# The output projection of a hybrid encoder layer, in two parts: the SSD's half of the contraction for all tokens, then the heads' half by token halves

## The chip, the core and the metric

The kernel runs on one core of a Trainium2 chip. A core has TensorE (PE: matmuls, with its weight loads listed as PEld), VectorE (DVE), ScalarE (ACT), GpSimd (POOL) and SyncE (SP, which only issues transfers here). Matmuls write PSUM, a small memory of eight banks; everything else lives in SBUF, and tensors too large for it lie in HBM and come and go by DMA. The metric is the device time of the whole program in microseconds.

## The reference

One inference step of one encoder layer over 2048 new frames of a prompt and 32 frames of a running stream, width 1024. The mixer reads the normalised input through one projection; half of the result goes to eight heads of stick-breaking attention, the other half to a Mamba-2 state-space part (SSD). Both results are normalised, laid side by side and go through one output projection; a gated feed-forward with a short convolution follows.

```python
attn = stick_breaking(q, q_pos, k_all, v_all, k_pos).reshape(b, l, D_ATT)      # D_ATT = 512
...
y = rmsnorm(y * jax.nn.silu(z), p['g_ssm_out'])                                # D_SSM = 512
out = jnp.concatenate([rmsnorm(attn, p['g_attn_out']), y], axis=-1) @ p['w_out']
...
m, k, v, h_fin, ssm_conv_new = mixer(rmsnorm(x, p['g_mix_pre']), ...)
x = x + rmsnorm(m, p['g_mix_post'])
f, ffn_conv_new = conv_ffn(rmsnorm(x, p['g_ffn_pre']), ffn_conv_prev, p)
x = x + rmsnorm(f, p['g_ffn_post'])
```

All of it is in 32-bit floats. The kernel gets that accuracy from a faster matmul format by splitting both operands into a high and a low part: each product is three matmuls (high x high, high x low, low x high).

## The kernel before

**Tiling.** Features lie on the 128 partitions, tokens along the free dimension. The tokens are cut into four super-blocks of 512, 512, 512 and 544 (`SBS`). A contraction over 1024 features is eight chunks k of 128; of the output projection's input `cat`, chunks 0 to 3 are the heads and 4 to 7 the SSD's result.

**Stages.** First, `phase_in` projects all super-blocks and does the SSD; the SSD's normalised result is stored to HBM (`yS`). Then `heads(s)` does the attention of super-block s in slots (head, key chunk, query block): score matmuls (line 811), sigmoids on ACT (659, 660), a scan on DVE (662), a product mostly on POOL (667), transposes on PE (832), a copy (835) and the value matmuls (847). Between slots, `fill` draws steps from a generator, the dense work of the super-block before: `Tail.stream`. A step is one call of `dense`, three matmuls on line 124. `count` says how many steps a stream has, and `heads` spreads them over its slots. For the last super-block there are no heads left, and its stream runs alone (`alone`), with three PSUM buffers instead of two and token tiles of 272.

**A stream**, in order: `norm_in` (called when the heads are done) loads the SSD's half of `cat` from `yS` into buffers that the previous stream's up matmuls read until their end (line 753), sums and roots the heads' squares, and writes the normalised heads in two token halves (759 to 761). Then eight steps of `owed`, the down projection's rest that the previous super-block left (32 steps of three matmuls of 512 columns; none at super-block 0). Then `out_units` for the first token half, then for the second, with the steps of `residual` for the first half strewn in, one after each fourth yield. Then the root of the first half, the residual of the second, `split` of both halves into the up projection's operands (958, 959), the rest of `owed`, and the feed-forward.

**The projection.** A unit of `out_units` is one output chunk c for one token half: eight steps, SSD chunks first, into one PSUM buffer, then an ACT copy into `m[c]` (924) and its square added to `msq` by ACT and POOL through one buffer `sqt` (771, 772). Each chunk's weights are one tile `w` of 1 MB, high and low parts; three such buffers exist (`WBUFS`). The second half starts with the last three chunks, whose weights are still there, and loads the other five again. At super-block 0 the weights come raw, are split by ACT and POOL (108, 109) and stored (`wS_out`); later they are loaded from there (104). `residual` loads the layer's input (`xr`, 939, two buffers), scales and adds (940, 944), stores the sum (945) and squares it.

**Order of the work.** The tile framework lays out each engine's queue from a simulated time line, so instructions can move against the program's order where nothing forbids it. `pin` and `mark` keep the dense matmuls behind the attention matmuls that stand before them in the program; attention matmuls are not held back by dense ones. SP's queue runs in order.

## Time and profile before

| | |
|---|---|
| median of 3 runs | 3005.11 us (2995.95 to 3006.34) |
| profiled execution | 2999.56 us, span of its instructions 2997.4 us, 43276 instructions |
| mean granted TensorE clock | 0.979 |
| PE busy | 2839.3 us, 95% of the span |
| DVE / ACT / POOL busy | 1567.7 / 1239.6 / 1254.8 us |
| moved by DMA | 571.58 MB, mean 191 GB/s |

The time of an execution is its span and a little over 2 us around it. A busy PE is not PE at its peak: matmuls overlap, and a matmul's row is longer than the distance to the next. The output projections' ACT copies (line 924) lie at 772.1 to 834.0, 1302.9 to 1355.6, 1880.1 to 1933.7 and 2478.7 to 2524.1 us.

### The profile page before, as it was taken

Reading aid. Unit: us, or ns where it says so; the run is one execution under the profiler, and the core shown is the slowest. Engines: PE = TensorE matmul, PEld = TensorE weight load, DVE = VectorE, ACT = ScalarE, POOL = GpSimd, SP = SyncE. Lnnn points to the kernel's source line nnn. Section 1 sums busy time; section 2 is a strip of 40 time slices with the busy share of each in tenths; the row PEclk is TensorE's granted clock in tenths of the full one; section 3 lists DMA queues with packets and bytes.
Section 4 is the critical chain, followed back from the end, with each engine's and each line's share of the span. In section 5 each row is a group of like instructions: output and inputs, shape, how many; then the busy total and the mean of one; then the engine's idle time right before and its main releaser. Section 6 shows DMA issues by size and latency. Waiting matters only on the chain.

```text
span 2997.4 us, 43276 instructions
## 1 busy us (share of the span) xinstructions
PE 2839.3 (95%) x16175; PEld 2320.3 (77%) x16175; DVE 1567.7 (52%) x2386; ACT 1239.6 (41%) x2514; POOL 1254.8 (42%) x1077
## 2 busy tenths in 40 slices
PE   8999899989979999999999999999999999899996
PEld 6777778866757778886677777856777779799996
DVE  7676676546574544337734344485444543523334
ACT  5344444346675544337533333564333433312111
POOL 4555555245666665536522222454122224511113
PEclk9999999989989999999999999999999999899998
DMA  5645453657657777876455545645544455554555
GB/s 172 183 145 177 144 169 106 185 150 248 241 178 242 246 250 266 289 265 203 158 190 176 184 156 208 232 163 174 177 165 167 157 196 191 192 188 167 178 178 171
DMA packets 234659, 571.58 MB, mean 191 GB/s; under 512 B 49514, under 2 KB 101362, under 8 KB 205906
## 3 DMA queue, kind: packets, MB, share of 16 engines
q1 hardware_dynamic: 234450, 568.81, 57.2%
q8 instruction: 129, 2.11, 0.3%
q14 instruction: 80, 0.66, 0.1%
HBM read 435.22 MB, written 133.50 MB: 190 GB/s over the span
## 4 chain that ended last, share of the span: by engine, by line
PE 72%; DVE 14%; DMA 6%; issue 3%; ACT 3%; POOL 2%; SPq 1%; DVEq 0%; POOLq 0%; ACTq 0%
PE o L124 36%; PE u L124 11%; PE t L124 10%; PE pa L847 4%; PE z L811 3%; PE pt L832 3%; DVE prow L662 2%; PE o L365 2%; DVE xc L341 2%; DVE acB L436 1%; DMA xr<-hS 1%; DMA acB<-acD 1%; DVE xc L337 1%; DVE x L263 1%; DMA w<-wS_out 1%
## 5 line engine op out<-in xcount | busy, mean ns | idle before, releaser
L124 PE MATMUL o<-xhi,w 128*128 128x512 f32 (+2 forms) x3968 | 1039.6, 346 | 28.4 <-ACT xhi L287 7.9
L124 PEld LDWEIGHTS o<-xhi,w 128*128 128x128 f32 x3968 | 696.5, 191 | 129.6 <-issue 10.1
L124 PE MATMUL o<-xlo,w 128*128 128x512 f32 (+2 forms) x1984 | 684.9, 345 | 9.4 <-DVE xlo L959 4.1
L109 POOL TENSOR_TENSOR w<-wraw,w 128x1024 fp32r<-128x1024 f32 (+2 forms) x156 | 370.6, 2376 | 256.1 <-ACT w L108 233.3
L124 PEld LDWEIGHTS o<-xlo,w 128*128 128x128 f32 x1984 | 379.6, 191 | 56.8 <-DVE xlo L959 7.6
L667 POOL TENSOR_TENSOR beta<-beta,prow 128x512 f32<-128x512 f32 (+3 forms) x256 | 255.7, 1000 | 377.4 <-DVE prow L662 345.2
L124 PE MATMUL u<-xhi,w 128*128 128x512 f32 x1056 | 345.8, 398 | 0.8 <-ACT r L201 0.5
L124 PE MATMUL o<-ah,w 128*128 128x512 f32 x992 | 335.9, 401 | 3.3 <-ACT f L1057 2.6
L1013 POOL TENSOR_TENSOR y<-y,gb 128x512 f32<-128x512 f32 (+1 forms) x88 | 115.5, 1313 | 511.2 <-ACT gb L1012 509.2
L662 DVE TENSOR_TENSOR_SCAN prow<-gam,prow,z 128x513 f32<-128x513 f32 x192 | 244.8, 1277 | 108.7 <-ACT beta L660 103.2
L124 PEld LDWEIGHTS u<-xhi,w 128*128 128x128 f32 x1056 | 198.5, 188 | 56.1 <-issue 5.6
L659 ACT ACTIVATE gam<-z 128x512 f32<-128x512 f32 (+2 forms) x320 | 173.3, 542 | 128.1 <-PE z L811 83.0
L124 PEld LDWEIGHTS o<-ah,w 128*128 128x128 f32 x992 | 187.1, 189 | 49.8 <-ACT f L1057 3.6
L124 PE MATMUL u<-xlo,w 128*128 128x512 f32 x528 | 209.3, 396 | 0.0
L835 ACT COPY wt<-pt 128x512 f32<-128x512 f32 (+3 forms) x282 | 148.1, 532 | 144.0 <-PE pt L832 141.3
L1005 DVE SCALAR_TENSOR_TENSOR y<-gb,cv,y 128x512 f32<-128x512 f32 (+1 forms) x176 | 162.3, 923 | 78.4 <-ACT y L1003 75.6
L108 ACT CAST w<-wraw 128x1024 fp32r<-128x1024 f32 (+2 forms) x156 | 155.2, 995 | 114.5 <-PE o L124 63.7
L124 PE MATMUL o<-al,w 128*128 128x512 f32 x496 | 196.5, 396 | 0.0
L124 PE MATMUL t<-xhi,w 128*128 128x272 f32 x960 | 189.1, 292 | 2.3 <-DMA w<-wS_up 2.0
L832 PEld LDWEIGHTS pt<-ident,beta 128*128 128x128 f32 x1088 | 132.4, 144 | 67.8 <-issue 27.5
L832 PE MATMUL pt<-ident,beta 128*128 128x128 f32 x1088 | 177.4, 282 | 6.4 <-POOL beta L667 3.9
L124 PE MATMUL t<-ah,w 128*128 128x272 f32 (+1 forms) x768 | 160.1, 302 | 17.4 <-ACT f L1057 7.5
(262 smaller groups left out, 4845.9 us busy)
## 6 DMA issues: line engine op xcount, KB each, us to landing
w<-wS_up SPq DMA_DIRECT2D x132, 1024.0 KB, 4.8
w<-wS_dn SPq DMA_DIRECT2D x72, 768.0 KB, 4.8
wS_up<-w SPq DMA_DIRECT2D x44, 1024.0 KB, 4.8
w<-wS_out SPq DMA_DIRECT2D x39, 1024.0 KB, 6.3
wraw<-wup SPq DMA_DIRECT2D x44, 512.0 KB, 5.9
k<-kS SPq DMA_DIRECT2D x80, 256.0 KB, 4.0
wS_dn<-w SPq DMA_DIRECT2D x24, 768.0 KB, 4.5
w<-wS_dn SPq DMA_DIRECT2D x32, 512.0 KB, 4.4
```

The lines of the kernel that those rows point to most:

```text
L108: nc.scalar.copy(hi[:, :n, :], raw[:, :n, :])
L109: nc.gpsimd.tensor_tensor(lo[:, :n, :], raw[:, :n, :], hi[:, :n, :].bitcast(F32), op=ALU.subtract)
L124: mm = nc.tensor.matmul(ps[:, : c1 - c0], l[:, k, :], at(r, k0 + k)[:, c0:c1], start=first and i == 0 and k == 0, stop=last and i == 2 and ...
L659: nc.scalar.activation(g[:, c0:512], z, AF.Sigmoid, scale=-0.125)
L662: nc.vector.tensor_tensor_scan(back(pr), back(g), z[:, 0:1].to_broadcast([P, n + 1]), self.kn.ones[:, 0:1] if prev is None else prev, op0= ...
L667: eng.tensor_tensor(b[:, :n], b[:, :n], pr[:, c0 + 1 : 513], op=ALU.mult)
L811: mm = nc.tensor.matmul(z[:, :n], q[:, P * b : P * b + P], k[:, :n], start=e == 0, stop=e == 1 and kc < s)
L832: mm = nc.tensor.transpose(t[:, P * j : P * j + P], w[:, P * j : P * j + P], kn.ident[:])
L835: copy(wt[:, : n // P, P * b : P * b + P], t[:, :n].rearrange("p (i q) -> p i q", q=P))
L847: nc.tensor.matmul(av[DH * (j % 2) : DH * (j % 2) + DH, c0:], v[:, j, :], wt[:, j, c0:], start=kc == s and j < 2, stop=kc == 0 and j > 1,)
L1005: nc.vector.scalar_tensor_tensor(y[:, :W], gb[:, i : i + W], kn.col(wc + i), y[:, :W], op0=ALU.mult, op1=ALU.add)
L1013: nc.gpsimd.tensor_tensor(y[:, :W], y[:, :W], t, op=ALU.mult)
```

## The change

`out_units` is cut in two. A new `out_ssd` runs first, over all tokens of the super-block in tiles of up to 512: for each output chunk four steps (SSD chunks 4 to 7), then an ACT copy into `m[c]`. It stands where the eight owed steps stood; all owed steps now come behind the split. `out_units` keeps the heads' four chunks by token halves; DVE adds their PSUM result to `m[c]` in place, and the squares follow. The weights are laid out anew, two output chunks' halves to a 1 MB tile: four tiles for the SSD (`wouts`), four for the heads (`wouta`), of which the second token half reloads one. Residual steps come after each second yield instead of each fourth, since the second half has half as many. `count` follows.

```diff
+    def out_ssd(self, s, cat):
+        kn, nc, att = self.kn, self.kn.nc, self.att
+        self.m = [self.mp.tile([P, 544], F32, name=f"m{c}") for c in range(KC)]
+        self.msq = att.tmp.tile([P, 544], F32, name="msq")
+        self.w = {}
+        for c in range(KC):
+            if c % 2 == 0:
+                w = kn.weight(kn.wp, kn.a["wouts"][c // 2], key=("outs", c // 2))
+            for c0, c1 in tiles_of(SBS[s][1]):
+                ps = self.po[0].tile([P, 512], F32, name=self.po[1])
+                for k in range(4):
+                    j = c % 2 * 4 + k
+                    kn.dense(ps, [t[:, j : j + 1, :] for t in w], cat, c0, c1, ks=1, k0=4 + k, first=k == 0, last=k == 3, pin=self.pin)
+                    if k < 3:
+                        yield
+                nc.scalar.copy(self.m[c][:, c0:c1], ps[:, : c1 - c0])
+                yield
...
     def out_units(self, s, cat, half):
...
-        back = list(range(KC - WBUFS, KC))
-        for i, c in enumerate(range(KC) if c0 == 0 else back + list(range(KC - WBUFS))):
...
-            for k in (4, 5, 6, 7, 0, 1, 2, 3):
...
-            nc.scalar.copy(m[:, c0:c1], ps[:, : c1 - c0])
-            att.square(self.msq[:, c0:c1], m[:, c0:c1], i == 0)
-            yield
+        for i, p in enumerate(range(4) if c0 == 0 else (1, 2, 3, 0)):
+            w = self.w.pop(p, None)
             if w is None:
+                pool = self.keep if self.keep is not None and p == 0 else kn.wp
+                w = kn.weight(pool, kn.a["wouta"][p], key=("outa", p), tag="w0" if pool is self.keep else None)
+                if c0 == 0 and (p or pool is self.keep):
+                    self.w[p] = w
+            for c in (2 * p, 2 * p + 1):
+                m = self.m[c][:, c0:c1]
+                ps = self.po[0].tile([P, 512], F32, name=self.po[1])
+                for k in range(4):
+                    j = c % 2 * 4 + k
+                    kn.dense(ps, [t[:, j : j + 1, :] for t in w], cat, c0, c1, ks=1, k0=k, first=k == 0, last=k == 3, pin=self.pin)
+                    if k < 3:
+                        yield
+                nc.vector.tensor_tensor(m, ps[:, : c1 - c0], m, op=ALU.add)
+                att.square(self.msq[:, c0:c1], m, i == 0 and c % 2 == 0)
+                yield
...
-        yield from islice(owed, 8)
+        yield from self.out_ssd(s, cat)
         yield from self.out_units(s, cat, a)
         chain = self.residual(s, a)
         for n, _ in enumerate(self.out_units(s, cat, b)):
             yield
-            if n % 4 == 0:
+            if n % 2 == 0:
                 next(chain, None)
...
-        return 2 * 8 * 8 + (2 * NJ * 8 + NJ * 8) * len(tiles_of(SBS[s][1])) - (32 if s == 0 else 0)
+        return 64 + (32 + 2 * NJ * 8 + NJ * 8) * len(tiles_of(SBS[s][1])) - (16 if s == 0 else 0)
...
+    def pairs(w):
+        return c(w.reshape(4, 2, P, 4, P).transpose(0, 2, 1, 3, 4).reshape(4, P, KC, P))
...
-        "wout": units(i["w_out"][0]),
+        "wouta": pairs(wout[:, :, :4]),
+        "wouts": pairs(wout[:, :, 4:]),
```

More of the change, by code (lines that the diff above doesn't have):

```diff
@@ L1 @@
 from contextlib import ExitStack
-from itertools import islice
 import concourse.bass as bass
@@ L905, in out_units @@
         c0, c1 = half
-        if c0 == 0:
-            self.m = [self.mp.tile([P, 544], F32, name=f"m{c}") for c in range(KC)]
-            self.msq = att.tmp.tile([P, 544], F32, name="msq")
-            self.w = {}
-        back = list(range(KC - WBUFS, KC))
-        for i, c in enumerate(range(KC) if c0 == 0 else back + list(range(KC - WBUFS))):
-            m = self.m[c]
-            w = self.w.pop(c, None)
-            if w is None:
-                pool = self.keep if self.keep is not None and c not in back else kn.wp
-                w = kn.weight(pool, kn.a["wout"][c], key=("out", c), tag=f"w{c}" if pool is self.keep else None)
-                if c0 == 0 and (c in back or pool is self.keep):
-                    self.w[c] = w
-            ps = self.po[0].tile([P, 512], F32, name=self.po[1])
-            for k in (4, 5, 6, 7, 0, 1, 2, 3):
-                kn.dense(ps, [t[:, k : k + 1, :] for t in w], cat, c0, c1, ks=1, k0=k, first=k == 4, last=k == 3, pin=self.pin)
-                if k != 3:
-                    yield
-            nc.scalar.copy(m[:, c0:c1], ps[:, : c1 - c0])
-            att.square(self.msq[:, c0:c1], m[:, c0:c1], i == 0)
-            yield
+        for i, p in enumerate(range(4) if c0 == 0 else (1, 2, 3, 0)):
+            w = self.w.pop(p, None)
+            if w is None:
+                pool = self.keep if self.keep is not None and p == 0 else kn.wp
[13 more added lines that the diff above has]
+                yield
     def residual(self, s, half):
@@ L1218, in fm @@
         return v.reshape(-1, P).T
+    def pairs(w):
+        return c(w.reshape(4, 2, P, 4, P).transpose(0, 2, 1, 3, 4).reshape(4, P, KC, P))
     i = {k: np.asarray(v) for k, v in inp.items()}
+    wout = units(i["w_out"][0])
     w_in = i["w_in"][0]
```

## The prediction

> **What bounds the kernel now.** I read the page's busy times first, then busy time by stretches around each output projection, then the same stretches for line 124 alone (the dense matmuls), then the PE timeline, the chain and the waits.
>
> ```profile
> PE 2839.3 (95%) x16175; PEld 2320.3 (77%) x16175; DVE 1567.7 (52%) x2386; ACT 1239.6 (41%) x2514; POOL 1254.8 (42%) x1077
> 1000.00:1250.00 250.00, 250.00 (x1115) 195.93 (x1115) 118.34 (x135) 108.56 (x191) 149.94 (x92) 1.00 0.75 258
> 736.00:763.00 27.00, 20.80 (x124) 13.26 (x123) 22.54 (x31) 19.92 (x44) 19.96 (x21) 1.00 0.55 182
> 763.00:806.00 43.00, 42.49 (x302) 36.75 (x303) 21.66 (x27) 29.54 (x70) 34.05 (x34) 0.92 0.67 242
> 834.00:876.00 42.00, 32.58 (x163) 18.55 (x161) 31.04 (x40) 30.10 (x72) 25.87 (x31) 0.88 0.53 169
> 1285.00:1297.00 12.00, 7.76 (x39) 6.20 (x38) 5.51 (x11) 3.42 (x8) 6.89 (x8) 0.93 0.99 341
> 1392.00:1425.00 33.00, 27.87 (x133) 17.64 (x134) 29.59 (x39) 25.21 (x59) 21.34 (x25) 0.90 0.48 151
> 1859.00:1870.00 11.00, 11.00 (x57) 8.00 (x56) 6.90 (x11) 4.52 (x11) 5.38 (x5) 1.00 0.95 337
> 1967.00:1997.00 30.00, 25.87 (x134) 15.95 (x134) 26.46 (x31) 22.12 (x53) 21.64 (x25) 1.00 0.60 185
> 2458.00:2470.00 12.00, 9.62 (x49) 6.70 (x47) 4.32 (x9) 3.32 (x8) 4.89 (x5) 0.98 1.00 385
> 2545.00:2578.00 33.00, 26.00 (x182) 25.14 (x181) 19.30 (x37) 14.57 (x33) 18.29 (x21) 0.90 0.51 171
> ```
>
> TensorE is the bound: in 1000 to 1250 us it never stops. It does stop around the four output projections, which I call stages 0 to 3. The columns are the stretch, its length, busy PE, PEld, DVE, ACT and POOL with counts, the granted clock, DMA share and GB/s. Now line 124 alone, in the same order of columns (PE and PEld only), and line 811, two score matmuls to an attention slot:
>
> ```profile
> 736.00:763.00 27.00, 0.49 (x3) 0.29 (x2) 1.00 0.55 182
> 834.00:876.00 42.00, 0.43 (x1) 0.19 (x1) 0.88 0.53 169
> 1000.00:1250.00 250.00, 226.68 (x952) 177.62 (x952) 1.00 0.75 258
> ...
> 736.00:763.00 27.00, 7.87 (x24) 3.61 (x24) 1.00 0.55 182
> 834.00:876.00 42.00, 11.45 (x34) 5.57 (x34) 0.88 0.53 169
> 1000.00:1250.00 250.00, 15.55 (x48) 7.71 (x48) 1.00 0.75 258
> ```
>
> So stage 0 has two long stretches in which the dense work stands still and attention alone runs: an opening, 736 to 763, and a closing, 834 to 876. The timeline says what the opening waits for: after the SSD part of the first unit, the next dense matmul waits for the normalised heads.
>
> ```profile
> 736.04 0.28 PE L124 MATMUL o<-xhi,w 128*128 128x256 f32 x1
> 762.82 0.56 PE L124 MATMUL o<-xhi,w 128*128 128x256 f32 x1 [0.82 <-ACT xhi L760]
> 1268.63 5.60 PE u L124 x24
> 1310.74 8.73 PE o L124 x72
> 2638.39 6.03 PE o L124 x48
> ```
>
> The last three rows are of the chain and price a matmul: 512 columns 5.60/24 = 0.233 us, 256 columns 8.73/72 = 0.121, 272 columns 6.03/48 = 0.126. A slot costs PE (250 - 952 x 0.233)/24 = 1.2 us.
>
> **The change part by part.**
>
> *Streaming.* Per stage 0 to 2, 384 matmuls of 256 columns become 96 of 512 and 192 of 256; stage 3 keeps its 384 of 272. 192 x 0.121 = 23.2 us against 96 x 0.233 = 22.4. The 256-column row includes a few gaps, so I take 0; the ends are 0 and 3 x 0.8 = -2.4.
>
> *Opening of stage 0.* The whole SSD half, 22.4 us, can now run while the heads are normalised. In 736 to 763 the 12 slots need 14 us of PE, so 13 of 27 us are free. The clock of 0.92 over the next 43 us costs 3.4 us more, and steady work should keep that. I take -15; the ends are 0 (the weights or the SSD operand late) and -16.4.
>
> *Closing of stage 0.* From the end of the first token half to the first up matmul runs a chain: sum of squares, root, residual, squares, root, residual, split. The second half's matmuls cover it, 22.4 us before, 11.2 after. What replaces them is attention, and in 834 to 876 its 17 slots used 20 of 42 us. So 11.2 us of lost cover cost 11.2 x 0.52 = +5.8; the ends are 0 and +11.2.
>
> *Openings of stages 1 to 3.* The eight owed steps (24 matmuls of 0.233 = 5.6 us) no longer stand ahead of the projection. The SSD operand lies in the buffers that the last up matmuls read, so its eight loads cannot start before:
>
> ```profile
> 1284.51 0.33 SPq L753 DMA_DIRECT2D xlo<-yS  x1
> 1287.35 1.17 SPq L753 DMA_DIRECT2D xlo<-yS  x2
> 1288.88 2.92 SPq L104 DMA_DIRECT2D w<-wS_out  x3
> 1286.42 0.40 PE L124 MATMUL u<-xhi,w 128*128 128x512 f32 x1
> 1296.80 0.58 PE L124 MATMUL o<-xhi,w 128*128 128x256 f32 x1 [3.78 <-DMA w<-wS_out]
> xlo<-yS SPq DMA_DIRECT2D x12, 256.0 KB, 5.0
> w<-wS_out SPq DMA_DIRECT2D x39, 1024.0 KB, 6.3
> ```
>
> Stage 1 waited for the weights, queued on SP behind these loads. After the change the first weight's buffer comes free a whole up unit earlier, so I expect its load ahead of the SSD operand, and the operand's landing to decide: some 2 to 7 us behind the last up matmul (1286.7). Stage 1 then idles about as long as now (0); stage 2, which has no idle time now (11.00 of 11.00), gains a gap of some 2.5 us and stage 3 of some 1, with a half-clock window for one of them, +1. Sum +4.5. The ends: each opening fully exposed, 3 x 5.6 = +16.8, or the present gaps gone, 4.2 + 2.4 = -6.6.
>
> The half clock is in the rows: behind the gap before 1296.80 the granted clock of 1285 to 1297 is 0.93, and 22 matmuls took 5.06 us:
>
> ```profile
> 1296.80 5.06 PE o L124 x22
> ```
>
> At 0.121 us they would take 2.7; the window cost 2.4 us. The Trainium skill (TensorE: Matmul & The Clock Gate, HAM oscillation) asks for no PE gaps above some 3.4 us, because behind one the clock halves. By that rule, which speaks against taking away the owed steps, three gaps of 5.6 us would each bring a half-clock window and the openings alone would cost 16.8 + 3 x 1.7 = 21.9 us, an estimate from that page's window; the trace agrees at 1296.80.
>
> *Closings of stages 1 to 3.* The owed steps now all stand behind the split: cover +5.6, but the second half's cover is -11.2. Net -5.6, half of it replaced by attention in stages 1 and 2: +2.8 each. Stage 3 has no attention: +5.6, less the slack in its chain, of which I count half: +3. Sum +8.6; the ends are -14.8 (the closings' idle time now, 5.1 in 1392 to 1425, 4.1 in 1967 to 1997 and 7.0 in 2545 to 2578, filled as far as 5.6 us each go) and +16.8.
>
> *Queues.* Second-half reloads shrink from five weights to one, so in all 39 loads become 27; the eight raw reads, casts and splits of the weights stay eight. Residual reads stand behind these loads on SP:
>
> ```profile
> SPq L104 <- PE o L124: 507.0, 116, 12.4
> L944 DVE TENSOR_TENSOR m<-m,xr 128x256 f32<-128x256 f32 x24 | 16.0, 665 | 24.6 <-DMA xr<-xT 24.6
> 821.65 8.18 DMA w<-wS_out
> ```
>
> In stage 0's chain of waits one such load takes 8.2 us. With fewer loads the residual of the first half comes sooner; attention would have used half of that time. I take -1.5 in each of stages 0 to 2, -4.5; the ends are 0 and 3 x 8.2 x 0.5 = -12. Stage 3 prefetches its residual: 0.
>
> *The add on VectorE.* 16 ScalarE copies a stage become 8 wider ones, and 16 VectorE adds come in:
>
> ```profile
> L924 ACT COPY m<-o 128x256 f32<-128x256 f32 x48 | 17.8, 371 | 53.6 <-PE o L124 53.4
> L1057 ACT COPY f<-o 128x512 f32<-128x512 f32 x24 | 14.1, 596 | 19.2 <-PE o L124 19.2
> L1059 DVE TENSOR_TENSOR f<-t,f 128x272 f32<-128x272 f32 x112 | 48.6, 440 | 61.8 <-PE t L124 61.7
> L662 DVE TENSOR_TENSOR_SCAN prow<-gam,prow,z 128x513 f32<-128x513 f32 x192 | 244.8, 1277 | 108.7 <-ACT beta L660 103.2 <-POOL fsq L772 1.5 <-POOL beta L667 1.3
> L772 POOL TENSOR_TENSOR msq<-msq,sqt 128x256 f32<-128x256 f32 x84 | 64.1, 764 | 61.1 <-ACT sqt L771 61.1
> ```
>
> ScalarE loses 16 x 0.371 - 8 x 0.596 = 1.2 us a stage, VectorE gains 16 x 0.44 = 7. A unit now has 12 matmuls, 1.45 us, on two banks. An add behind a scan comes after 1.28 + 0.44 = 1.72 us, 0.27 late; and while it waits for its unit, the scans behind it wait, and with them the scores of later slots. At most 16 x 0.27 = 4.3 us a stage in stages 0 to 2; I take +2.5 in all, between 0 and +13. The squares keep their number but come twice as close, every 1.45 us, where ScalarE and POOL hand over one buffer: POOL's 0.76 and ScalarE's 0.42 fit just so while the residual's squares stay away. In the second half these join, 16 items of at least 1.2 us in 11.2 us; that lateness is in the chains above.
>
> *Sum.* 0 - 15 + 5.8 + 4.5 + 8.6 - 4.5 + 2.5 = +1.9 us. The profiled execution took 2999.56 us (span 2997.4), so 3001.5; the median of the runs shown, 3005.11, is 5.5 above that execution, and their spread is 2995.95 to 3006.34. I forecast 3001. Half a per cent, 15 us, is about what a measurement of this kernel can tell from no change.
>
> **The rivals.**
>
> *Faster: the closings do not care for cover.* If the chain behind the first half is paced by residual reads and by squares, which attention on ScalarE and POOL slows, and not by the second half's matmuls, it starts earlier in stage 0 and ends earlier, and the owed steps fill what is idle behind the splits. Then the opening gives -16.4, the closings -14.8 instead of +14.4, the reads -4.5, with the openings +4.5 and the adds +2.5 as before: 2999.6 - 28.7 = 2971. For it speaks the read of 8.2 us in the chain; against it that stage 0 has no owed steps at all and that its closing ran on attention alone, at half of PE's use. Chance 0.28.
>
> *Slower: the openings are exposed.* Without the eight steps PE stands still from the last up matmul until the SSD operand has landed, three times 5.6 us and each time a half-clock window of 2.4: 24.0 instead of 4.5, so 3021. It decides once all three gaps reach about 5 us. For it speaks that the loads' issue is tied to the last up matmuls, 1284.5 to 1288.5, with 5.0 us to landing. Against it: the present wait was for a weight behind these loads, and attention has PE work at stage 2's opening. Chance 0.16.
>
> *The change does not do what it says in stage 0.* If weight splits or the operand are late, the SSD half runs after 763 all the same: no -15, 3016. POOL is busy 20 of 27 us there, and four weights must be split; two weights suffice for the first 11 us. Chance 0.12.
>
> **How the numbers follow.** The forecast itself, 0.44, has a range of 2990 to 3012 from terms that are uncertain by some 5 us each. The 0.8 range reaches into the other cases: 2972 to 3022 leaves out the far ends of the faster case and of the exposed openings. Faster by over 0.5%: the first rival nearly whole and a little of the forecast's edge, 0.29. Slower by over 0.5%: the exposed openings and two thirds of the unfilled opening, 0.24. Within: 0.47.
>
> **What would show it.** Right: line 124 runs in 736 to 763, some 90 of its matmuls at 512 columns, and the wait on xhi L760 goes; the stretch with one dense matmul behind stage 0's second half gets longer; loads of projection weights are 27; the closings of stages 1 and 2 show 24 more matmuls on ah behind the split. Wrong: gaps of over 5 us ended by the SSD operand (xhi or xlo from yS) at three openings; a matmul group waiting on DVE m often; or stage 0's first up matmul before about 850 us, which would mean that its chain needs no cover.

## The result, and the profile after

The changed kernel takes 3022.72 us (median of 5 runs, 3013.47 to 3026.95) where the kernel before took 3002.99 (median of 5 runs, 2995.95 to 3006.34): ratio 1.0065, 95% interval 1.005 to 1.008. It is slower by 0.65%. The forecast was 3001, with a range up to 3022.

The profiled execution after took 3022.72 us, its span is 3020.9. First the page's busy times, then the projection weights' rows of the page's DMA part (source and tile, queue, count, size, median us to landing), then TensorE's three rows of the waits that matter below.

```profile
PE 2853.1 (94%) x15887; PEld 2315.0 (77%) x15887; DVE 1596.6 (53%) x2450; ACT 1237.1 (41%) x2490; POOL 1257.3 (42%) x1077
...
w<-wS_outa SPq DMA_DIRECT2D x15, 1024.0 KB, 4.8
w<-wS_outs SPq DMA_DIRECT2D x12, 1024.0 KB, 4.8
...
PE z L810 <- DVE prow L661: 30.2, 33, 3.4
PE pt L831 <- DVE beta L666: 7.6, 6, 4.5
PE o L123 <- DMA xhi<-yS: 4.7, 3, 2.1
```

The 27 loads are there. VectorE has 29 us more to do. TensorE waits longer for the scans than before (23.4 us then), and its waits for the SSD operand at the openings are short. (Lines moved up by one: 123 is the dense matmul, 661 the scan, 810 the score. New are 917, the copy of the SSD half, and 939, the add; the residual's scaling and adding are now 955 and 959.)

The span grew by 23.5 us. TensorE's idle time, the span less its busy time, grew from 158.1 to 167.8 us. The mean granted clock fell from 0.979 to 0.975, which is worth 62.9 us of the span before and 75.5 us after (an estimate: one minus the clock, times the span). So about half of the loss is idle time, 9.7 us, and about half a lower clock, 12.6 us.

**Lining the two traces up.** Because work moved, equal times mean nothing. I added up the columns of all matmuls in each trace, at 0.2333 us per 512 columns (the prediction's row, 5.60/24). Both sums are 2586.9 us. Then I took the times at which 590, 610, 730, 1080, 1300, 2120 and 2280 us of such work had begun: between two marks both kernels do the same amount of matmul work, though not the same matmuls. In us:

| between the marks | before | after | difference |
|---|---|---|---|
| start to 590 (`phase_in`, the first heads) | 728.5 | 731.2 | +2.7 |
| 590 to 610 (opening of stage 0) | 41.9 | 34.0 | -7.9 |
| 610 to 730 (rest of stage 0's projection, closing, first up) | 164.5 | 184.1 | +19.6 |
| 730 to 1080 (up and down) | 367.0 | 366.7 | -0.3 |
| 1080 to 1300 (stage 1) | 262.7 | 273.4 | +10.7 |
| 1300 to 2120 (with stage 2) | 894.5 | 891.4 | -3.1 |
| 2120 to 2280 (stage 3) | 194.2 | 195.9 | +1.7 |
| 2280 to the end | 344.1 | 344.2 | +0.1 |

The sum is 23.5 us, the difference of the spans. The first row is one of chance: TensorE's order is the same, but for one pair of matmuls, up to about 705 us, and in twenty executions of all kernels here, lined up in this way, it took 723.6 to 737.1 us. So stage 0 costs 11.7 us, stage 1 10.7, and the rest is small.

Two cautions. First, the mark at 610 lies badly: in the kernel after it falls at 765.2 us, in the middle of a stop of the dense work that lasts until 779.5 (below). With the mark at 615, behind that stop, the second row is 55.2 us before and 59.4 after, +4.2, and the third +7.4. So the -7.9 is not a gain; only the sum of the two rows can be relied on. Second, columns underprice attention. In 1000 to 1250 us of the kernel before, where TensorE never stops, they come to 243.4 us, so each of the 24 slots there takes some 0.28 us more than its columns say (an estimate). Stage 1's row holds 13 scans more after the change and the next row 13 fewer, so some 3.6 us of the +10.7 are only moved there from the next row, and stage 1 loses nearer 7.

The next fence gives the rows of the busy times by stretches for the second, third and fifth row of that table, kernel before first, then the scans alone in the same stretches (stretch, length, busy VectorE with the number of scans, clock, DMA share, GB/s). Then the same for the kernel after.

```profile
728.50:770.40 41.90, 33.84 (x207) 24.13 (x206) 34.01 (x56) 31.16 (x72) 32.08 (x34) 0.92 0.58 197
770.40:934.90 164.50, 148.04 (x871) 113.11 (x870) 95.60 (x120) 102.50 (x230) 105.37 (x105) 0.95 0.65 220
1301.90:1564.60 262.70, 249.68 (x1346) 189.60 (x1346) 148.04 (x203) 135.98 (x311) 122.73 (x138) 0.98 0.59 196
...
728.50:770.40 41.90, 16.98 (x16) 0.92 0.58 197
770.40:934.90 164.50, 42.96 (x41) 0.95 0.65 220
1301.90:1564.60 262.70, 59.47 (x52) 0.98 0.59 196
```

```profile
731.20:765.20 34.00, 30.41 (x173) 20.78 (x172) 23.09 (x42) 22.61 (x49) 24.22 (x24) 0.90 0.70 235
765.20:949.30 184.10, 158.57 (x844) 112.16 (x844) 123.11 (x163) 119.41 (x271) 115.10 (x122) 0.93 0.52 169
1316.00:1589.40 273.40, 255.95 (x1308) 186.77 (x1307) 171.57 (x236) 149.94 (x336) 138.91 (x154) 0.97 0.53 174
...
731.20:765.20 34.00, 12.21 (x12) 0.90 0.70 235
765.20:949.30 184.10, 60.34 (x57) 0.93 0.52 169
1316.00:1589.40 273.40, 74.13 (x65) 0.97 0.53 174
```

Read the scans. In the rest of stage 0 stand 57 scans where 41 stood, in stage 1's stretch 65 where 52 stood. Attention, which nothing holds back, runs ahead while the dense work stands; and where it runs alone TensorE is not full. In the third row of the table TensorE is idle for 184.1 - 158.6 = 25.5 us against 164.5 - 148.0 = 16.5 before, and the granted clock is 0.93 against 0.95.

Now the opening of stage 0. Line 123 alone (busy PE and PEld), then rows of the timeline on PE, ACT and DVE:

```profile
736.00:763.00 27.00, 5.50 (x21) 3.54 (x21) 0.92 0.68 232
763.00:778.00 15.00, 0.00 (x0) 0.00 (x0) 0.61 0.42 145
...
741.80 0.40 PE L123 MATMUL o<-xhi,w 128*128 128x512 f32 x1
770.37 0.80 PE L810 MATMUL z<-k,qa 128*128 128x512 f32 x1 [3.38 <-DVE prow L661]
778.36 0.79 PE L810 MATMUL z<-k,qa 128*128 128x512 f32 x1 [1.39 <-DVE fhist L898]
779.47 0.78 PE L123 MATMUL o<-xhi,w 128*128 128x512 f32 x1
777.39 1.01 ACT L759 CAST xhi<-att 128x256 fp32r<-128x256 f32 x3
778.30 1.07 ACT L917 COPY m<-o 128x512 f32<-128x512 f32 x2
778.26 0.10 DVE L898 MEMSET fhist<- 128x44 f32 x1
```

Two units of the SSD half run, until 742.2, and fill both banks. Their copies (917) come at 778.30, in ScalarE's queue behind the cast of the normalised heads (759); between stand the scores of 16 slots. The dense work restarts at 779.47, after a clock of 0.61 in 763 to 778; in the kernel before it restarted at 762.82. The memset of `fhist`, the first instruction that the tail issues, comes at the same moment as the copies: that pointed to the memory of the tail's tiles.

Events of the program show stage 0 without any mark inside the stop. Each fence line below is the scans' row of a stretch: first from the 590 mark to the end of the last projection matmul (833.0 and 846.1 us), then from there to the first up matmul (875.6 and 897.3). Kernel before, then after:

```profile
728.50:833.00 104.50, 29.64 (x28) 0.97 0.71 246
833.00:875.60 42.60, 18.12 (x17) 0.88 0.53 169
...
731.20:846.10 114.90, 32.48 (x31) 0.90 0.59 197
846.10:897.30 51.20, 24.25 (x23) 0.93 0.45 144
```

The projection ends 10.4 us later than before, at a clock of 0.90 instead of 0.97, and the closing behind it is 8.6 us longer, with 23 scans instead of 17. By the first up matmul some 7.7 us more of matmul work, attention's, is done, which brings these 19.0 us down to about the table's 11.7.

### The profile page after: what moved, and what is told of

Read it like the earlier page. It is cut to its first block, busy times and chain, and to the rows that moved or that the text cites. A ratio compares the mean times of both kernels' runs of the same rounds, so it can differ in the third digit from the quotient of the medians.

```text
span 3020.9 us, 42752 instructions
## 1 busy us (share of the span) xinstructions
PE 2853.1 (94%) x15887; PEld 2315.0 (77%) x15887; DVE 1596.6 (53%) x2450; ACT 1237.1 (41%) x2490; POOL 1257.3 (42%) x1077
## 4 chain that ended last, share of the span: by engine, by line
PE 61%; DVE 6%; DMA 5%; ACT 2%; POOL 2%; issue 2%; SPq 0%; DVEq 0%; ACTq 0%; POOLq 0%
PE o L123 29%; PE u L123 11%; PE t L123 10%; PE pa L846 4%; PE z L810 3%; PE pt L831 3%; DVE prow L661 2%; DMA wraw<-wup 1%; DVE m L955 1%; DMA xr<-xT 1%; DVE f L1095 1%; DVE y L1020 1%; DMA w<-wS_dn 1%; DVE xlo L974 1%; DMA xr<-hS 0%
## 5 line engine op out<-in xcount | busy, mean ns | idle before, releaser
L123 PEld LDWEIGHTS o<-xhi,w 128*128 128x128 f32 x3776 | 675.5, 192 | 131.0 <-issue 10.3
L123 PE MATMUL o<-xlo,w 128*128 128x512 f32 (+2 forms) x1888 | 669.9, 355 | 9.4 <-DVE xlo L272 3.6
L123 PEld LDWEIGHTS o<-xlo,w 128*128 128x128 f32 x1888 | 362.6, 192 | 62.0 <-DVE xlo L974 6.8
```

Of the source, the lines that this page charges most:

```text
L123: mm = nc.tensor.matmul(ps[:, : c1 - c0], l[:, k, :], at(r, k0 + k)[:, c0:c1], start=first and i == 0 and k == 0, stop=last and i == 2 and ...
```

## The experiments

Each ratio is to the kernel before, timed beside it, and is worked out from all runs, so it can differ a little from that of the medians. The lengths between the marks are in a table at the end of the section.

**The memory of m.** *e1_home*: the tail's pools are entered in another order, so that most of `m` and `fhist` no longer lie over the last SSD tiles.

```diff
-        self.mp = pool("tl_m", 1, side="right")
         self.gp = pool("tl_g", 4, side="right")
         self.yp = pool("tl_y", 2, side="right")
         self.rp = pool("tl_r", 2, side="right")
+        self.mp = pool("tl_m", 1, side="right")
```

> The four pools of the tail are entered in another order, so that the tiles m (and f, fhist) lie above the memory of the last SSD tiles; instructions and their order stay as in the changed kernel. Theory A (the copies of the SSD half into m waited in stage 0 for the memory of the last SSD tiles, and with two PSUM banks full the dense matmuls stood from 742 to 779.5 us): the SSD half now runs on in the opening, dense matmuls and line 917 between 742 and 775 us, stage 0's up matmuls 10 to 16 us earlier, 3007 to 3013 us, ratio to before 1.001 to 1.0035. Rival B (stage 0 is late for its weights, its operand or VectorE's adds): the memset of fhist goes early, but the time stays at 3020 to 3025, ratio 1.006 to 1.0075.

Measured: 3024.59 us, 1.0053 (1.0035 to 1.0072). The order of instructions had stayed the same on every engine, and so did the picture (ScalarE's timeline in that kernel):

```profile
772.26 1.00 ACT L759 CAST xhi<-att 128x256 fp32r<-128x256 f32 x3
773.17 1.07 ACT L917 COPY m<-o 128x512 f32<-128x512 f32 x2
```

So the address alone is not it: the copies stand behind the cast in a queue whose order is fixed. *e15_left* opens `m`'s pool ahead of the closing of the SSD's pools, in the place of the sampled tokens' tiles.

```diff
-        kp = ctx.enter_context(kn.tc.tile_pool(name="as_k", bufs=2, reuse_waits="tile", side="right"))
+        kp = ctx.enter_context(kn.tc.tile_pool(name="as_k", bufs=2, reuse_waits="tile"))
...
+        kn.mm = mm(own)          # pool "tl_mm"; closed and opened again ahead of stage 3
         for _ in normed:
             pass
         ssd.close()
...
-        self.m = [self.mp.tile([P, 544], F32, name=f"m{c}") for c in range(KC)]
+        self.m = [kn.mm.tile([P, 544], F32, name=f"m{c}") for c in range(KC)]
```

> The tiles m get memory of their own, in the place of the sampled tokens' tiles, whose use ends at about 745 us, and not over the last SSD tiles; in the built order the eight copies of line 917 of stage 0 now stand ahead of the first xhi copy of line 759, where before six of them stood behind it. Theory A2 (the memory of the last SSD tiles holds up the SSD half in stage 0, through the order made for it: in the first try, with the pools in another order and the same order of instructions, nothing moved): units 3 to 8 run ahead of 765 us, the opening gives back 10 to 15 us, 3007 to 3013 us, ratio 1.0015 to 1.0035. Rival B2 (the opening is limited by the scans and the norm on VectorE, and the dense work is only taken away from a later place that is bare): SSD half early in the trace, time 3018 to 3024, ratio 1.005 to 1.007, with more or longer gaps in the closing of stage 0.

Measured: 3021.54 us, 1.0066 (1.0048 to 1.0084). ScalarE's timeline, line 123 alone in the old opening, then the first two of the stretches between the marks with all engines and with the scans alone, and last the scans in the two stretches up to and behind the last projection matmul:

```profile
740.58 1.07 ACT L917 COPY m<-o 128x512 f32<-128x512 f32 x2
764.20 0.59 ACT L917 COPY m<-o 128x512 f32<-128x512 f32 x1
769.06 0.40 ACT L759 CAST xhi<-att 128x256 fp32r<-128x256 f32 x1
...
736.00:763.00 27.00, 19.30 (x77) 13.97 (x76) 1.00 0.66 226
...
727.40:751.20 23.80, 23.55 (x137) 17.96 (x136) 12.00 (x28) 14.83 (x28) 15.85 (x15) 1.00 0.68 232
751.20:933.50 182.30, 159.03 (x870) 110.74 (x868) 131.74 (x170) 123.32 (x280) 123.80 (x128) 0.95 0.56 185
...
727.40:751.20 23.80, 5.55 (x5) 1.00 0.68 232
751.20:933.50 182.30, 62.54 (x59) 0.95 0.56 185
...
727.40:818.10 90.70, 23.88 (x22) 0.98 0.61 213
818.10:876.20 58.10, 27.09 (x26) 0.91 0.54 177
```

This is the picture that the prediction drew: 77 dense matmuls in 736 to 763, the eight copies ahead of the cast, full clock. Between the marks the opening falls from 41.9 to 23.8 us, 18.1 less, and the stretch behind it grows from 164.5 to 182.3, 17.8 more. By the events, which are the safer ends, the projection ends 13.8 us earlier than before (90.7 against 104.5) and the closing is 15.5 us longer (58.1 against 42.6, 26 scans against 17). The opening had not been empty: 16 scans ran there, now 5 do, and the rest of stage 0 has 59 where it had 41. Theory A2 is right on the hold-up and wrong on what it is worth; in stage 0 rival B2 is right. (This profiled execution, 3015.22, is the fastest of the kernel's six, so its total says less than its stretches.)

*e17_before_left* gives the kernel before the same memory.

> The kernel before with m's own memory alone. If the memory also held up stage 0 there (its dense matmuls stood at 742 to 763): up to 6 us earlier, 2995 to 3000 us, ratio 0.9975 to 0.999. If its stop was the heads' operand (xhi of line 760): no change, 2999 to 3007, ratio 0.999 to 1.0015.

Measured: 3005.6 us, 1.0014 (1.0002 to 1.0027): no gain. Its stretches differ by at most 1.6 us from those of the kernel before, except the first. That flatters what one trace is worth: two executions of one and the same kernel (f2_split1 and g2_split1_again, below) agree within 2.2 us from 590 to 1300, but differ by 7.6 us in 1300 to 2120 and by 5.7 in stage 3. So smaller differences in these last two stretches say nothing by themselves.

**Where the loss is made.** *e6_old0* puts stage 0 back to whole units, *e7_old123* stages 1 to 3, both from the new weight arrays, two transfers a tile.

```diff
...
+        old = s in (0,)          # e7_old123: (1, 2, 3)
+        units = self.old_units if old else self.out_units
+        yield from islice(owed, 8) if old else self.out_ssd(s, cat)
...
```

> Stage 0 alone is put back to whole units of eight steps by token halves, evacuated by ScalarE, from the same two weight arrays (each weight tile comes by two transfers); stages 1 to 3 stay split. If the loss is made in stage 0 (Theory A or B: 8 to 15 us): 3008 to 3014, ratio 1.0015 to 1.004. If it is made behind it (Theories C, D): 3018 to 3024, ratio 1.005 to 1.007.

> Stage 0 stays split; stages 1 to 3 are put back to whole units, with the eight owed steps ahead of them (weights by two transfers a tile out of the stored arrays). If stages 1 to 3 made about 12 us of the loss (Theories C, D): 3008 to 3013, ratio 1.0015 to 1.0035, and with the run with stage 0 put back the two gains add up to about 20. If all of it is stage 0 (Theory A alone, with the trace's 12 us in stage 1 only a shift of stalls that another execution wouldn't show): 3018 to 3024.

Measured: e6_old0 3016.12 us, 1.0034 (1.0021 to 1.0047); e7_old123 3023.79, 1.0066 (1.0045 to 1.0088). Putting stage 0 back gains something, putting stages 1 to 3 back nothing. But both kept the changed kernel's `count`, so that a stage of whole units got 624 steps' pace for 656 steps (608 for 624 in stage 0). Hence:

**The pace.** *e10_steps* counts each step of the SSD half twice and uses the old `count`; *e13_before_pace* is the kernel before with the new `count`; *e16_left_steps* is e10_steps with m's own memory.

```diff
# e10_steps, in out_ssd, and count() as before
                     kn.dense(ps, ...)
+                    yield
                     if k < 3:
                         yield
```

> Only the pace of the filler is put back: each step of the SSD half counts as two (an empty step beside it), and the number of steps that sets the rate is that of the kernel before (656 for stages 1 and 2, 624 for stage 0), so that a slot of the heads gets 9.75, 6.83 and 5.125 steps as before, not 9.5, 6.5 and 4.875. Theory E (the loss of stage 1, which also stayed where stages 1 to 3 had whole units but the new number of steps, comes from fewer filler steps per slot while the heads wait for their scans): 3008 to 3014 us, ratio 1.002 to 1.004, the 12 us of stage 1 gone. Rival D (the closing itself, squeezed residual steps on VectorE): 3019 to 3026, ratio 1.005 to 1.007.

> The kernel before with the changed kernel's number of steps alone (624 where it has 656, 608 where it has 624). Theory E: the same loss as in the changed kernel's stage 1 and some in stage 0, 3011 to 3019 us, ratio 1.003 to 1.005. Rival D: nothing, 2999 to 3007, ratio 0.999 to 1.001.

> Both edits, m's own memory and the pace of before. A2 and E: the two gains add up, 2994 to 3003 us, ratio 0.997 to 1.000. One of them alone: 3007 to 3014. Neither (B2 and D): 3018 to 3026.

Measured: 3028.97 us, 1.0086 (1.0069 to 1.0103); 3010.03, 1.0025 (1.0015 to 1.0035); 3015.24, 1.0048 (1.0031 to 1.0064). The pace costs 0.25% in the old order, so the kernel is that sensitive to it; but put back in the new order it mends nothing. With m's own memory beside it (e16_left_steps) the median is 6 us below e15_left's, with intervals that overlap, and far above the 3003 of the case that both gains add up. Theory E falls as the cause. *g1_count* corrects the one number in the change that is off: at stage 0 nothing is owed, 32 steps less, and the change takes off 16.

```diff
-        return 64 + (32 + 2 * NJ * 8 + NJ * 8) * len(tiles_of(SBS[s][1])) - (16 if s == 0 else 0)
+        return 64 + (32 + 2 * NJ * 8 + NJ * 8) * len(tiles_of(SBS[s][1])) - (32 if s == 0 else 0)
```

> The changed kernel with stage 0's number of steps put to the 592 that it has (608 were said, so its filler ended some 1.7 slots before the heads). Theory K (the wrong number shifts the slots of the stages behind): 3006 to 3014 us, ratio 1.001 to 1.004, and fewer than 60 scans in the stretch of stage 1. Rival G (the closings lack cover whatever the number): 3018 to 3026, ratio 1.005 to 1.008, 61 to 65 scans there and stage 0's closing longer by 7 to 9 us as before.

Measured: 3022.59 us, 1.0062 (1.0045 to 1.0078). Theory K falls: the rest of stage 0 takes 183.5 us, stage 1 270.3 with 61 scans.

**Cover for the openings, pace of the residual.** *e2_owed8* puts the eight owed steps back ahead of the SSD half; *e4_pace* strews the first half's residual half as densely, the rest behind the loop.

```diff
+        yield from islice(owed, 8)                    # e2_owed8
         yield from self.out_ssd(s, cat)
...
-            if n % 2 == 0:
+            if n % 4 == 0:                            # e4_pace
                 next(chain, None)
+        for _ in chain:
+            yield
```

> Eight steps of the down projection that is owed stand ahead of the SSD half again, as before the change. Theory C (the openings of stages 1 to 3 are exposed: gaps of 2.1, 1.05 and 2.0 us before xhi and xlo, and half clock for 10.2 and 3.4 us, worth 5.2 + 6.8 = 12 us): the gaps on the operand go and the time falls by 8 to 12, to 3011 to 3015, ratio 1.0025 to 1.004. Rival D (the loss of stage 1 lies in the closing and behind it, on VectorE): the same work only changes its place, 3020 to 3027, ratio 1.006 to 1.008, with longer gaps where the owed steps are missing at the closing.

> The steps of the first half's residual come at each fourth step of the second half, not each second, and the rest of them behind it. If the squeezed residual (VectorE's row of eight in 834 to 840 us and the gap of 4.48 us behind it) makes the loss of the closing: 5 to 8 us back, 3014 to 3018. Theory G: the closing only ends later, 3022 to 3032, ratio 1.006 to 1.010.

Measured: 3036.07 us, 1.0098 (1.0082 to 1.0114); 3037.44, 1.0119 (1.0099 to 1.014). Both are worse than the change, by a third and by half a per cent. Eight steps taken from behind the split and put at the opening make stage 1's stretch 280.6 us (273.4 in the change). But e2_owed8 is no clean test of cover: its waits for the operand at the openings of stages 1 and 2 are gone, and in their place its dense work waits 5.0 us at stage 1 (at 1309.7 us) and 2.5 at stage 2 (1909.4) for weights of the SSD half, more than the 5.5 us of waits for the operand that the change has at these two openings. And of the 7.2 us in stage 1's stretch one wait of 3.6 us, at 1379.4 us, is for an add of VectorE (`m`). So it shows that putting the steps back does not help, not that dense work is worth more in the closing. A later residual makes the rest of stage 0 3.8 us longer than in the change.

**VectorE's adds or the missing cover.** *e3_act* leaves the adding of the SSD half out: the heads' half is copied over it by ScalarE.

```diff
-                nc.vector.tensor_tensor(m, ps[:, : c1 - c0], m, op=ALU.add)
+                nc.scalar.copy(m, ps[:, : c1 - c0])
```

> The 64 evacuations of the heads' half are ScalarE copies that overwrite m; the SSD half is computed and copied but not added (left out). Theory F (VectorE's adds, 9.6 us more of tile m in the stretch of stage 1 in which the loss is made, delay the scans): the adds gone, 8 to 12 us back, 3008 to 3014 us, ratio 1.002 to 1.004. Rival G (the dense work of the SSD half is spent in the opening and is missing as cover in the closing, where now 65 scans stand where 52 stood and TensorE waits for them): 3018 to 3026, ratio 1.005 to 1.008, with about as many scans in that stretch.

Measured: 3018.46 us, 1.005 (1.0034 to 1.0066). By the medians 4 us of 20 went, with intervals that overlap. In the trace stage 0's two stretches together are 4.0 us shorter than in the change and stage 1's 4.6. In stage 1's stretch stand 57 scans, 8 fewer than in the change, so some 2 us of the 4.6 are moved by the price of a slot. The adds are a part, the smaller one, and not clear of noise.

*e18_half* leaves the closings their dense work: the SSD half goes first for the first token half alone, the second half is whole units again, at the old pace, with the owed steps as before and m's own memory. *f4_half0_left* does that in stage 0 only, the other stages in whole units.

```diff
-            for c0, c1 in tiles_of(SBS[s][1]):                 # out_ssd
+            for c0, c1 in ((0, SBS[s][1] // 2),):
...
-        for n, _ in enumerate(self.out_units(s, cat, b)):      # stream
+        for n, _ in enumerate(self.whole_units(s, cat, b)):
```

> The SSD half goes first for the first token half alone, with m's own memory; the second half is done in whole units of eight steps by ScalarE copies behind it, with the pace and the eight owed steps of before, so that the closing has all its old cover. Theory G: the loss goes and about half of the opening's gain stays: 2992 to 3002 us, ratio 0.9965 to 1.0005; fewer than 56 scans in the stretch of stage 1. Rival F or H (the split itself costs: 32 adds on VectorE, more and smaller evacuations, more weight transfers): 3008 to 3016, ratio 1.002 to 1.005.

> In stage 0 alone the SSD half goes first for the first token half only, with m's own memory; the second half and all other stages in whole units at the pace of before. Theory G (the closing keeps its dense work): 2996 to 3001 us, ratio 0.998 to 0.9997, the best of the kernels by about the 3 us that stage 0 gained in the run with half the split everywhere. Rival: the same as before, 3001 to 3006.

Measured: 3014.11 us, 1.0041 (1.0026 to 1.0056), and 3005.3 us, 1.0005 (0.9991 to 1.0018). Half of the early work costs 0.41% where all of it costs 0.65%; stage 1's share of it is 6.4 us, with 56 scans. 9.9 of the 16.2 us by which this trace is longer are in stage 3, where the dense work waits 2.2 and 1.7 us for weights that are queued behind my loads of whole tiles; the rest is about what two executions differ by there. In stage 0 alone it is the kernel before, no better. Between the marks the opening gives 15.3 and the rest takes 17.8; by the events the projection ends only 3.8 us earlier, and the closing is 4.5 us longer.

**Each stage by itself.** At the right pace (but for the 608 steps of the change that stage 0 of f1 and f3 keeps), the stages not named in whole units: *f1_split0* splits stage 0 only, *f2_split1* stage 1 only, *f3_split0_left* stage 0 with m's own memory; *g2_split1_again* is f2_split1 once more.

```diff
+        old = s in (1, 2, 3)     # f1, f3; f2, g2: (0, 2, 3)
...
+        if s in (1, 2, 3):       # count(): 656 steps there, the new number in a split stage
+            return 2 * 8 * 8 + (2 * NJ * 8 + NJ * 8) * len(tiles_of(SBS[s][1])) - (32 if s == 0 else 0)
```

> Split in stage 0 alone, as in the changed kernel; stages 1 to 3 in whole units, with the number of steps of before (656) and the eight owed steps. Theory I (each stage's split costs by itself): stage 0's 10 to 12 us only, 3011 to 3015 us, ratio 1.003 to 1.0045, and nothing more in the trace behind 930 us. Rival J (a shift of the slots in stage 0 or the two transfers a tile, not the split, makes stage 1 lose): 3020 or more, ratio 1.006 and up.

> Split in stage 1 alone (624 steps there); stages 0, 2 and 3 in whole units with the numbers of steps of before. Theory I with G: 10 to 12 us in stage 1 and some 61 to 65 scans in its stretch, 3011 to 3016 us, ratio 1.003 to 1.005. Rival J: 3000 to 3006, ratio 0.9995 to 1.0015.

> The kernel with stage 1 alone split, once more. If the first profile tells the loss rightly (11 us between 1360 and 1500 us, in the closing of stage 1, and nothing behind it): the same stretch again, 262.7 us before against 272 to 275, with 64 scans. If the loss moves from execution to execution: another place or under 6 us there. The median: 3014 to 3023 us.

> Split in stage 0 alone, with m's own memory, so that the SSD half fills the opening. If the opening's gain (17 us in the run with that memory) is given back in the closing of stage 0, as there: 3000 to 3006 us, ratio 0.9995 to 1.0015. If it is the memory that cost and the split is a gain: 2990 to 2996, ratio 0.996 to 0.998.

Measured: f1_split0 3023.62 us, 1.0069 (1.0047 to 1.0091); f2_split1 3021.38, 1.0064 (1.0047 to 1.008); g2_split1_again 3024.22, 1.0066 (1.0047 to 1.0085); f3_split0_left 3020.42, 1.0055 (1.0037 to 1.0073). Stage 1's stretch with its scans in f2_split1, g2_split1_again, f4_half0_left and f3_split0_left:

```profile
1303.40:1576.60 273.20, 72.99 (x64) 0.97 0.54 175
```

```profile
1316.70:1589.60 272.90, 73.02 (x64) 0.97 0.54 175
```

```profile
1305.20:1565.30 260.10, 58.44 (x51) 0.99 0.60 198
```

```profile
1303.00:1577.30 274.30, 60.73 (x53) 0.96 0.56 185
```

The split of stage 1 by itself costs 10.5 and 10.2 us there, in two executions (3009.88 us, the fastest of f2's six, and 3037.27, the slowest of g2's), and brings 12 scans more; some 3.4 us of it are again those slots' price. In f2 and g2 stage 0, though of whole units, opens 7.1 and 9.0 us late; e6_old0, which also splits its raw weights from two transfers a tile, opens 4.5 late. So their medians hold a cost of my edit beside stage 1's. What I cannot explain is f1 and f3: behind a split stage 0, stage 1 in whole units takes 267.7 and 274.3 us at the old number of scans, where the same code behind f4's stage 0 takes 260.1. f1 meets the 3020 of rival J; of its two reasons the two transfers a tile fall out, since f4 has them in stage 1 too. Something carries over from stage 0; what, stays open. It also means that the costs do not add up: by the medians stage 0 alone (f1, f3) or stage 1 alone (f2, g2) costs about as much as the whole change.

Lengths between the marks of one profiled execution each:

| kernel | to 590 | to 610 | to 730 | to 1080 | to 1300 | to 2120 | to 2280 | ratio |
|---|---|---|---|---|---|---|---|---|
| before | 728.5 | 41.9 | 164.5 | 367.0 | 262.7 | 894.5 | 194.2 | 1 |
| e17_before_left | 733.7 | 43.0 | 162.9 | 366.7 | 263.8 | 893.5 | 193.6 | 1.0014 |
| e13_before_pace | 730.4 | 42.1 | 162.8 | 368.2 | 266.0 | 895.8 | 197.8 | 1.0025 |
| after | 731.2 | 34.0 | 184.1 | 366.7 | 273.4 | 891.4 | 195.9 | 1.0065 |
| e1_home | 727.3 | 32.0 | 183.0 | 364.2 | 272.3 | 892.1 | 195.3 | 1.0053 |
| e15_left | 727.4 | 23.8 | 182.3 | 368.6 | 272.4 | 896.0 | 197.5 | 1.0066 |
| e16_left_steps | 727.6 | 24.6 | 185.1 | 365.3 | 273.5 | 897.0 | 196.6 | 1.0048 |
| e10_steps | 730.6 | 31.7 | 186.5 | 367.9 | 275.6 | 895.2 | 196.1 | 1.0086 |
| g1_count | 737.1 | 31.5 | 183.5 | 366.3 | 270.3 | 894.1 | 197.0 | 1.0062 |
| e2_owed8 | 731.1 | 33.1 | 183.6 | 366.8 | 280.6 | 894.5 | 200.0 | 1.0098 |
| e4_pace | 728.9 | 31.6 | 187.9 | 363.6 | 274.3 | 900.6 | 202.2 | 1.0119 |
| e3_act | 723.6 | 32.4 | 181.7 | 369.3 | 268.8 | 893.7 | 194.8 | 1.0050 |
| e18_half | 731.8 | 26.2 | 179.0 | 365.6 | 269.1 | 894.6 | 204.1 | 1.0041 |
| f4_half0_left | 729.8 | 26.6 | 182.3 | 366.5 | 260.1 | 894.6 | 196.8 | 1.0005 |
| e6_old0 | 731.6 | 46.4 | 161.4 | 367.1 | 273.6 | 890.7 | 195.4 | 1.0034 |
| e7_old123 | 728.4 | 31.8 | 183.5 | 366.5 | 272.0 | 895.2 | 197.5 | 1.0066 |
| f1_split0 | 725.6 | 31.7 | 186.7 | 366.6 | 267.7 | 899.0 | 193.7 | 1.0069 |
| f3_split0_left | 726.3 | 24.3 | 183.2 | 369.2 | 274.3 | 902.9 | 195.1 | 1.0055 |
| f2_split1 | 723.7 | 49.0 | 163.2 | 367.5 | 273.2 | 896.2 | 191.5 | 1.0064 |
| g2_split1_again | 733.1 | 50.9 | 165.4 | 367.3 | 272.9 | 903.8 | 197.2 | 1.0066 |

## Why the prediction was wrong

**The opening of stage 0 is the step that failed first: -15 expected, a loss found.** "The whole SSD half can now run while the heads are normalised" did not happen: two of its eight units ran, then the dense work stood from 742.2 to 779.5 us. With the mark behind that stop the opening costs 4.2 us, and the projection ends 10.4 us later. This is 19 of the 21 us by which stage 0 was missed (-15 + 5.8 = -9.2 forecast, +11.7 found), and 21 us is nearly the whole miss. I asked whether operand and weights would be there, and they were: 24 matmuls ran by 742.2. I did not ask where their results go. Their copies into `m` stand in ScalarE's queue behind the cast of the heads. The order laid out follows the memory of `m`: e15_left, in which `m` has its own, has the copies ahead of the cast. My rival "the change does not do what it says in stage 0" has the place right, with 3016, but its reasons, late weights or a late operand, are not the ones.

**The closing of stage 0 is the step that would have failed all the same.** I charged lost cover at 0.52 of its length (+5.8), because attention would stand in its place, and I booked the opening's gain beside it as if the two were independent. In the change the closing is 8.6 us longer, inside my ends of 0 and 11.2. But with the hold-up gone (e15_left) the projection ends 13.8 us earlier, so my -15 was nearly right in size, and the closing is 15.5 us longer, far from +5.8 and outside the ends. They are one account: nine scans more stand in that closing, and up to the 730 mark nothing is left of the gain. The row to see it was in my first fence: 22.5 of 27 us of VectorE were busy in the opening. The squeezed residual that I had noted shows up as one row of eight on VectorE with a transpose waiting behind it (timeline of the kernel after):

```profile
834.04 5.89 DVE L955 SCALAR_TENSOR_TENSOR m<-m,cv,rstd 128x256 f32<-128x256 f32 x8
840.68 1.09 PE L831 MATMUL pt<-ident,beta 128*128 128x128 f32 x4 [4.48 <-DVE beta L666]
```

**The rest came out right in sum, in part by luck.** Openings, closings, queues and adds were to give 4.5 + 8.6 - 4.5 + 2.5 = +11.1. The stretches from 730 on give -0.3 + 10.7 - 3.1 + 1.7 + 0.1 = +9.1, but otherwise spread, and two executions of one kernel differ by almost as much. A lower clock, half of the whole loss, stands in my sum only at the openings of the stages (in stage 0 as a gain).

- *Streaming*: not measured. Both traces hold 2586.9 us of matmul work, but columns are counted there, which the change does not alter; it says nothing of their price.
- *Openings of stages 1 to 3*: the waits for the operand are 3.5 us at stage 1 (3.8 before, for a weight; I had no difference), 2.0 at stage 2 (I had 2.5) and none at stage 3 (I had 1). The rival of exposed openings is wrong though its 3021 was met: it needs three gaps of 5.6, and no wait for the operand is longer than 2.1 at once. A right number is no proof of its reason.
- *Closings*: stage 1's stretch costs +10.7 where I had +2.8, but it holds more than the closing. From the last projection matmul to the first up matmul it takes 47.9 us (1375.8 to 1423.7) against 37.2 before (1355.1 to 1392.3). The 24 matmuls more of owed steps in it, which I forecast, are 5.6 of these 10.7 us, so at most 5.1 us are lost there, with 14 scans where 10 stood. For the other two no size can be given: all of 1300 to 2120 gives -3.1, all of stage 3 +1.7, both less than what two executions differ by.
- *Queues*: 27 loads, and VectorE's wait for the residual reads fell, in the groups by line, from the 24.6 us that the prediction quoted to 4.4 (first row; the second is the add of the last item):

```profile
L959 DVE TENSOR_TENSOR m<-m,xr 128x256 f32<-128x256 f32 x24 | 14.8, 615 | 4.4 <-DMA xr<-xT 4.4
L939 DVE TENSOR_TENSOR m<-o,m 128x256 f32<-128x256 f32 x48 | 19.8, 412 | 29.5 <-PE o L123 29.3
```

  But only half of the residual's adds run on VectorE; GpSimd's wait for the same reads, on the same line, grew from 11.4 to 15.6. No gain in time can be seen from it.
- *The adds*: 412 ns each, as estimated from the 440 of the down projection's. Their effect, +2.5 with an end at +13, is more like 4 (medians of e3_act) to 9 (its trace, 4.0 + 4.6, less some 2 for the slots that moved), within my ends and not clear of noise.

The faster rival, closings that need no cover, is refuted in stage 0: its sign was a first up matmul before about 850 us, and that one comes at 897.3 in the change and at 876.2 in e15_left, behind the longer closings. Of the signs of being right, the 27 loads and the 24 more owed matmuls in stage 1's closing came; the 90 dense matmuls in 736 to 763 did not (21).

What is shown: the hold-up of the copies into `m` in stage 0, its size, and that the gain without it is given back in the same stage; that stage 1's stretch is 10 us longer with stage 1 alone split, twice; that the kernel with the second token half's units whole, and a split in stage 0 alone (f4_half0_left), keeps the time of before. Only argued: that attention running ahead is what costs. The scans go with the loss in stages 0 and 1 where these are split, but f3_split0_left loses in stage 1 without more scans. Open: what carries over from a split stage 0, and how much of the 20 us each stage makes. No version beat the kernel before.

## What to carry to other kernels

Before counting dense work as a gain in a hole, ask what else ran in that hole and where it goes: here, with the hold-up gone, a projection that ended 13.8 us earlier was followed by a closing 15.5 us longer, with the attention that had run in the hole. For each step that is moved earlier, check its output's tile as well as its inputs: when is it handed out, and does the laid-out order already reflect that? And compare traces with moved work by equal amounts of work, not by equal times; put no mark inside a stop, check against events of the program, and look at a second execution of one kernel before reading a few microseconds.

## What was unexpected of the hardware

The page that the prediction named for the clock (the Trainium skill, TensorE: Matmul & The Clock Gate, HAM oscillation) asks for no gaps above some 3.4 us. Here the clock also fell behind a shorter one, of 2.07 us; the kernel after, its timeline on PE and then the busy times of a stretch, with the granted clock behind the five engines:

```profile
1382.14 0.50 PE L123 MATMUL o<-ah,w 128*128 128x512 f32 x1 [2.07 <-DVE f L1074]
...
1380.00:1400.00 20.00, 17.93 (x80) 11.53 (x80) 18.18 (x24) 14.05 (x32) 15.47 (x16) 0.91 0.74 237
```

The gap is all the idle time of the stretch (20.00 - 17.93), and 0.91 over 20 us is 1.8 us of clock lost. So this short gap cost nearly twice its own length.
